# Loads of the modulation's weights on GpSimd's queue instead of SyncE's

## The chip, the cores and the metric

The kernel runs on one core of a Trainium2 chip. The core has TensorE (PE, matrix products), VectorE (DVE), ScalarE (ACT), GpSimd (POOL) and SyncE (SP), which work in parallel, each through its own instructions in a fixed order, and wait for each other on semaphores. Data comes from the chip's memory by DMA; an engine's queue issues a DMA, and the core's 16 DMA engines carry it out. The metric is device time in microseconds (us) of one execution. Everything is in 32-bit floats.

## The reference

One block of a network works on 256 rows of width 2048 in three sublayers. Each sublayer is wrapped in the same way:

```
h = modulate(rms_norm(x, gain_pre), shift, scale)      # h * (1 + scale) + shift
y = rms_norm(fn(h), gain_post)
x = x + weight * (1 + gate) * y
```

The first and the third `fn` are feed-forward layers, `(silu(h @ w_gate) * (h @ w_up)) @ w_down`, with an inner width of 5632. The second is a mixer: `h @ w_in`, then a pooling branch on 512 columns and a recurrent branch (24 heads of size 64, with decay) on the rest, joined and multiplied by `w_out`.

The shifts, scales and gates are the modulation. They are nine vectors of 2048 (three for each sublayer), all from one product of a single row with a large matrix:

```
mod = (silu(c) @ w_ada + b_ada).reshape(B, 3, 3, D_MODEL)
```

`w_ada` is 2048 x 18432, 151 MB. Nothing in it depends on `x`, so its columns can be read at any time before the vector they make is needed.

## The kernel before

**Matrix products.** Each 32-bit weight tile is split into a high and a low part (`split`, lines 173 to 184): ScalarE writes `hi` (line 179), VectorE writes `lo = raw - hi` (line 180), and TensorE sums three products of the parts (lines 189 to 191, 196 and 197, or 523 to 525). A weight tile, `raw`, is loaded by `load` (line 169) on SP's queue, mostly 1 MB at a time. There are four such buffers in the feed-forward layers and two in the mixer. A buffer is free again when line 180 has read it.

**The modulation.** It does not use TensorE for the large product. `ada_step` (lines 220 to 265) handles a quarter of the 2048 rows of `w_ada` for one task. A task is 1024 columns of one vector (two tasks a vector), except for the first two vectors, shift and scale of the first sublayer, whose tasks hold the same columns of both, in five blocks of growing width. For each group of 128 rows the step loads a tile of 128 x 1024 numbers (512 KB, line 235; for the first two vectors 256 KB pieces, line 238) and VectorE adds it, scaled by `silu(c)`, to an accumulator (line 242 for the first, line 244 for the others). At the end of a task VectorE transposes and sums the accumulator, and small products on TensorE finish it (lines 246 to 265). The tiles are called `ada`; there are four such buffers in the feed-forward layers and two in the mixer.

**When the steps run.** The order of the vectors is set in `begin` (line 1163): `(1, 0)` first, then 2, 4, 3, 5, 7, 6, 8. `ada_end` holds the step at which each one ends, and `ada_pos` is the step that is next; the first two vectors take 20 steps of four row groups, each of the seven others 8 steps. Calls of `tick` (lines 616 and 749) after the loads of weights start a step every so many loads, by the constants `ADA_FFN1`, `ADA_MIXER`, `ADA_OUT`, `ADA_FFN2`; `ada_finish` (line 267) runs the missing steps before a vector is needed.

**Stages.** The first feed-forward layer (to about 800 us) reads most of the modulation beside its own weights. The mixer follows (to about 1400 us), then the second feed-forward layer, which has loads of the modulation only at its start.

**What sets the order.** The program is written as one sequence with priorities. A planner of the framework lays out the order in which each engine and each queue gets its instructions, by these priorities, its own estimates of durations, and free buffers. On the chip each queue then works strictly in this order: SP's queue holds the loads of weights and those of the modulation, and a load that waits for its buffer holds back all loads behind it. ScalarE's queue issues a few small loads. GpSimd's queue issues none.

Of the kernel before, what the change touches and what calls it, by code (L numbers as in the profile page):

```python
# [18 lines left out]
D = 2048  # L19
# [57 lines left out]
class Block:  # L77
# [142 lines left out]
    def ada_step(self, psum):  # L220
        nc = self.nc
        if self.ada_pos == len(self.ada_tasks):
            return
        cols, k0 = self.ada_tasks[self.ada_pos]
        width = cols[0][2]
        (v0, c0, _), (v1, c1, _) = cols
        per = 512 // width
        if k0 == 0:
            self.acc = self.tile(self.accs, [P, 2, width], tag="acc")
        acc = self.acc  # L230
        for kk in range(k0, k0 + 4, per):
            raw = self.tile(self.raws, [P, per, 2, width], tag="ada", bufs=self.ada_bufs)
            w = self.I["w_ada"][kk * P:(kk + per) * P, :].rearrange("(k p) c -> p k c", p=P)
            if (v0, c0 + width) == (v1, c1):
                nc.sync.dma_start(raw.rearrange("p k j c -> p k (j c)"), w[:, :, v0 * D + c0:v0 * D + c0 + 2 * width])
            else:
                for j, (v, c, _) in enumerate(cols):
                    nc.sync.dma_start(raw[:, :, j, :], w[:, :, v * D + c:v * D + c + width])
            for i in range(per):
                ck = self.csilu[:, kk + i:kk + i + 1]  # L240
                if kk + i == 0:
                    self.later(nc.vector.tensor_scalar(acc, raw[:, i], ck, None, ALU.mult))
                else:
                    self.later(nc.vector.scalar_tensor_tensor(acc, raw[:, i], ck, acc, ALU.mult, ALU.add))  # L244
        self.ada_pos += 1
        if k0 == KD - 4:
            n = width // P
            ps = self.tile(psum, [P, 512], tag="mm")[:, :2 * n]
            if v0 != v1:
                for i in range(2 * n):  # L250
                    nc.tensor.matmul(ps[:, i:i + 1], acc[:, i // n, i % n * P:(i % n + 1) * P], self.ones[:, :1],
                                     start=True, stop=True)
            else:

                flip = self.tile(self.raws, [P, 2 * width], tag="ada", bufs=self.ada_bufs)
                nc.vector.transpose(flip, acc.rearrange("p j c -> p (j c)"))
                sums = self.tile(self.small, [P, 2 * n, 4], tag="sums")
                nc.vector.tensor_reduce(sums.rearrange("p k q -> p (k q)"), flip.rearrange("p (b t) -> p b t", t=32),
                                        mybir.AxisListType.X, ALU.add)
                for q in range(4):  # L260
                    nc.tensor.matmul(ps[32 * q:32 * q + 32, :], self.quads, sums[:, :, q], start=True, stop=True)
            for j, (v, c, _) in enumerate(cols):
                for a, m, ap in self.columns("b_ada", v * KD + c // P, n):
                    nc.vector.tensor_tensor(self.mod[:, v, c // P + a:c // P + a + m], ps[:, j * n + a:j * n + a + m],
                                            ap, ALU.add)
# [1000 lines left out]
```

## Time and profile before

| | us |
|---|---|
| median of 3 runs | 2158.49 (2156.7 to 2158.58) |
| the profiled execution | 2157.36 |
| its span | 2155.6 |
| TensorE busy | 2072.4 |
| VectorE busy | 1621.2 |
| ScalarE busy | 1079.1 |
| GpSimd busy | 0.2 |

The profile is of one execution. In its rows L169 is line 169 of the kernel; `lo L180` is the instruction of line 180 that writes the tile `lo`; `SPq` is SP's queue, and `A <- B` in a table of waits means that A waited for B, with the total in us, how often, and the longest. In groups, `x224` is a count, and three numbers with slashes are the shortest, median and longest duration in ns. TensorE's busy time is modelled from its pipelined products. The chain of waits is the work that ended last, followed back step by step to what released it. A row of busy time by stretches gives the length, the busy us and instructions of each engine, the granted TensorE clock, the share of time in which the DMA engines moved data, and GB/s.

### The profile page before, as it was taken

Reading aid. Unit: us, or ns where it says so; the run is one execution under the profiler, and the core shown is the slowest. Engines: PE = TensorE matmul, PEld = TensorE weight load, DVE = VectorE, ACT = ScalarE, POOL = GpSimd, SP = SyncE. Lnnn points to the kernel's source line nnn. Section 1 sums busy time; section 2 is a strip of 40 time slices with the busy share of each in tenths; the row PEclk is TensorE's granted clock in tenths of the full one; section 3 lists DMA queues with packets and bytes.
Section 4 is the critical chain, followed back from the end, with each engine's and each line's share of the span. In section 5 each row is a group of like instructions: output and inputs, shape, how many; then the busy total and the mean of one; then the engine's idle time right before and its main releaser. Section 6 shows DMA issues by size and latency. Waiting matters only on the chain.

```text
span 2155.6 us, 37182 instructions
## 1 busy us (share of the span) xinstructions
PE 2072.4 (96%) x14955; PEld 1802.4 (84%) x14955; DVE 1621.2 (75%) x2523; ACT 1079.1 (50%) x1823; POOL 0.2 (0%) x4
## 2 busy tenths in 40 slices
PE   4999999999999998899999999999999999999998
PEld 3999988888888877888887866799888888888887
DVE  6788898798877778899998877788755555555556
ACT  4534543444433455765656654665434444444453
POOL 0000000000000000000000000000000000000000
PEclk8999999999999999999999979999999999999999
DMA  9999888999888748845644526599755555555553
GB/s 317 359 315 322 289 282 306 323 336 315 304 308 294 277 141 243 258 140 173 192 137 147 182 81 195 169 311 320 254 195 194 180 193 196 187 185 195 194 181 133
DMA packets 316570, 502.31 MB, mean 233 GB/s; under 512 B 12037, under 2 KB 197486, under 8 KB 316142
## 3 DMA queue, kind: packets, MB, share of 16 engines
q1 hardware_dynamic: 314380, 496.32, 68.6%
q10 hardware_dynamic: 2018, 3.62, 0.5%
q8 instruction: 117, 1.92, 0.4%
q14 instruction: 55, 0.45, 0.1%
HBM read 497.77 MB, written 2.12 MB: 232 GB/s over the span
## 4 chain that ended last, share of the span: by engine, by line
PE 83%; DMA 7%; DVE 6%; ACT 3%; issue 2%; SPq 0%; DVEq 0%; ACTq 0%
PE mm L196 21%; PE mm L197 10%; PE mm L191 7%; PE mm L190 7%; PE mm L189 7%; PE mm L523 7%; PE mm L525 7%; PE mm L524 7%; DMA ada<-in_w_ada_dram 5%; DVE lo L180 2%; DVE acc L244 1%; DMA raw<-in_w_in_dram 1%; ACT hi L179 1%; PE sb L1110 1%; PE sb L1145 0%
## 5 line engine op out<-in xcount | busy, mean ns | idle before, releaser
L179 ACT CAST hi<-raw 128x1024 fp32r<-128x1024 f32 (+2 forms) x768 | 694.6, 911 | 780.7 <-PE mm L525 266.9
L180 DVE TENSOR_TENSOR lo<-raw,hi 128x1024 fp32r<-128x1024 f32 (+2 forms) x768 | 796.4, 1048 | 351.6 <-ACT hi L179 348.5
L196 PE MATMUL mm<-hT,hi 128*128 128x512 f32 x1984 | 698.6, 395 | 0.0
L197 PE MATMUL mm<-hT,lo 128*128 128x256 f32 x1984 | 558.3, 281 | 2.4 <-DVE lo L180 2.4
L196 PEld LDWEIGHTS mm<-hT,hi 128*128 128x128 f32 x1984 | 373.8, 188 | 87.9
L244 DVE SCALAR_TENSOR_TENSOR acc<-ada,csilu,acc 128x1024 f32<-128x1024 f32 (+1 forms) x285 | 349.0, 1225 | 96.7 <-DMA ada<-in_w_ada_dram 94.7
L190 PE MATMUL mm<-hT,hi 128*128 128x256 f32 x1376 | 395.0, 288 | 3.4 <-DVE hT L362 3.4
L189 PE MATMUL mm<-hT,hi 128*128 128x256 f32 x1376 | 392.0, 289 | 4.0 <-ACT hT L357 3.8
L191 PE MATMUL mm<-hT,lo 128*128 128x256 f32 x1376 | 393.2, 287 | 0.5 <-DVE lo L180 0.5
L197 PEld LDWEIGHTS mm<-hT,lo 128*128 128x128 f32 x1984 | 372.8, 188 | 3.3 <-DVE lo L180 3.1
L189 PEld LDWEIGHTS mm<-hT,hi 128*128 128x128 f32 x1376 | 260.9, 191 | 10.6 <-ACT hT L357 6.1
L190 PEld LDWEIGHTS mm<-hT,hi 128*128 128x128 f32 x1376 | 261.9, 190 | 9.1 <-DVE hT L362 5.5
L191 PEld LDWEIGHTS mm<-hT,lo 128*128 128x128 f32 x1376 | 261.9, 191 | 4.5 <-DVE lo L180 0.7
L523 PE MATMUL mm<-hi,act 128*128 128x512 f32 (+1 forms) x688 | 264.9, 385 | 0.0
L524 PE MATMUL mm<-lo,act 128*128 128x512 f32 (+1 forms) x688 | 264.5, 384 | 0.0
L525 PE MATMUL mm<-hi,act 128*128 128x512 f32 (+1 forms) x688 | 264.4, 384 | 0.0
L524 PEld LDWEIGHTS mm<-lo,act 128*128 128x128 f32 x688 | 129.3, 188 | 25.9 <-DVE lo L180 0.6
L525 PEld LDWEIGHTS mm<-hi,act 128*128 128x128 f32 x688 | 129.3, 188 | 25.7
L523 PEld LDWEIGHTS mm<-hi,act 128*128 128x128 f32 x688 | 129.3, 188 | 25.6
L641 ACT ACTIVATE silu<-silu 128x512 f32<-128x512 f32 x31 | 19.6, 632 | 58.0 <-DVE silu L640 58.0
L644 ACT CAST act<-silu 128x512 fp32r<-128x512 f32 x31 | 19.2, 618 | 31.1 <-DVE silu L642 31.1
L606 DVE TENSOR_TENSOR act<-act,mm 128x512 f32<-128x512 f32 x48 | 32.2, 681 | 1.8 <-PE mm L191 1.6
(371 smaller groups left out, 1936.2 us busy)
## 6 DMA issues: line engine op xcount, KB each, us to landing
ada<-in_w_ada_dram SPq DMA_DIRECT2D x224, 512.0 KB
raw<-in_ffn_w_down_dram SPq DMA_DIRECT2D x88, 1024.0 KB
raw<-in_ffn_w_gate_dram SPq DMA_DIRECT2D x84, 1024.0 KB
raw<-in_ffn_w_up_dram SPq DMA_DIRECT2D x84, 1024.0 KB
raw<-in_w_in_dram SPq DMA_DIRECT2D x34, 1024.0 KB
ada<-in_w_ada_dram SPq DMA_DIRECT2D x128, 256.0 KB
raw<-in_w_out_dram SPq DMA_DIRECT2D x16, 1024.0 KB
raw<-in_w_in_dram SPq DMA_DIRECT2D x9, 512.0 KB
```

Of the source, the lines that this page charges most:

```text
L179: a = nc.scalar.copy(hi, raw)
L180: d = nc.vector.tensor_tensor(lo, raw, hi.bitcast(F32), ALU.subtract)
L189: nc.tensor.matmul(ps, hi, x[:, 0, :], start=start, stop=False)
L190: nc.tensor.matmul(ps, hi, x[:, 1, :], start=False, stop=False)
L191: nc.tensor.matmul(ps, lo, x[:, 0, :], start=False, stop=stop)
L196: nc.tensor.matmul(ps.rearrange("p a t -> p (a t)"), hi, x.rearrange("p a t -> p (a t)"), start=start, stop=False)
L197: nc.tensor.matmul(ps[:, 0, :], lo, x[:, 0, :], start=False, stop=stop)
L244: self.later(nc.vector.scalar_tensor_tensor(acc, raw[:, i], ck, acc, ALU.mult, ALU.add))
L523: nc.tensor.matmul(ps, x[:, 0, ts], hi, start=start, stop=False)
L524: nc.tensor.matmul(ps, x[:, 0, ts], lo, start=False, stop=False)
L525: nc.tensor.matmul(ps, x[:, 1, ts], hi, start=False, stop=stop)
L606: nc.vector.tensor_tensor(part, part, bank, ALU.add)
```

## The change

`ada_step` chooses the queue for its loads. While the position is before the end of the first two vectors, `(1, 0)`, the loads stay on SP's queue. From then on GpSimd's queue issues them. The tiles, their buffers, the instructions that use them and the places of the steps in the program are as before.

```
         for kk in range(k0, k0 + 4, per):
             raw = self.tile(self.raws, [P, per, 2, width], tag="ada", bufs=self.ada_bufs)
+
+            queue = nc.sync if self.ada_pos < self.ada_end[(1, 0)] else nc.gpsimd
             w = self.I["w_ada"][kk * P:(kk + per) * P, :].rearrange("(k p) c -> p k c", p=P)
             if (v0, c0 + width) == (v1, c1):
-                nc.sync.dma_start(raw.rearrange("p k j c -> p k (j c)"), w[:, :, v0 * D + c0:v0 * D + c0 + 2 * width])
+                queue.dma_start(raw.rearrange("p k j c -> p k (j c)"), w[:, :, v0 * D + c0:v0 * D + c0 + 2 * width])
             else:
                 for j, (v, c, _) in enumerate(cols):
-                    nc.sync.dma_start(raw[:, :, j, :], w[:, :, v * D + c:v * D + c + width])
+                    queue.dma_start(raw[:, :, j, :], w[:, :, v * D + c:v * D + c + width])
```

## The prediction

> **What bounds the kernel now.** I read the page of the profile first, then busy time by stretches of 50 us, then the waits of three places.
>
> ```profile
> PE 2072.4 (96%) x14955; PEld 1802.4 (84%) x14955; DVE 1621.2 (75%) x2523; ACT 1079.1 (50%) x1823; POOL 0.2 (0%) x4
> ...
> PE 83%; DMA 7%; DVE 6%; ACT 3%; issue 2%; SPq 0%; DVEq 0%; ACTq 0%
> ```
>
> TensorE is busy for 96% of the span and holds 83% of the chain that ended last; SP's queue holds 0%. GpSimd does nothing. The change works on the queue that nobody waits for by this account, so the first question is where TensorE is idle at all.
>
> ```profile
> 0.00:50.00 50.00, 18.15 (x91) 15.96 (x92) 33.80 (x61) 20.83 (x34) 0.20 (x4) 0.89 0.93 312
> ...
> 450.00:500.00 50.00, 50.00 (x291) 43.33 (x290) 44.48 (x51) 24.57 (x32) 0.00 (x0) 1.00 0.96 332
> ...
> 650.00:700.00 50.00, 47.55 (x252) 40.23 (x252) 38.77 (x40) 19.05 (x24) 0.00 (x0) 0.97 0.82 288
> ...
> 800.00:850.00 50.00, 43.12 (x309) 36.76 (x308) 43.77 (x95) 33.96 (x77) 0.00 (x0) 1.00 0.73 222
> 850.00:900.00 50.00, 42.46 (x349) 39.76 (x349) 38.73 (x67) 31.30 (x62) 0.00 (x0) 1.00 0.84 268
> ...
> 950.00:1000.00 50.00, 48.98 (x621) 43.23 (x608) 46.50 (x117) 29.58 (x76) 0.00 (x0) 1.00 0.51 156
> ...
> 1400.00:1450.00 50.00, 45.65 (x363) 44.03 (x363) 41.83 (x55) 32.94 (x52) 0.00 (x0) 0.97 0.92 320
> ...
> 1600.00:1700.00 100.00, 100.00 (x557) 86.92 (x556) 53.83 (x58) 45.99 (x57) 0.00 (x0) 1.00 0.58 190
> ```
>
> The columns after the length are busy us of PE, PEld, DVE, ACT and POOL, then the granted clock, the DMA share and GB/s. Of 2155.6 - 2072.4 = 83.2 us without TensorE, 31.9 lie in the first 50 us, where the modulation loads that stay on SP are read. The first feed-forward layer runs at 50.00 of 50 with the DMA engines at 0.96; the second, from 1600 us, at 100 of 100 with no modulation left. The stretches that the change can reach and that are not full are 650 to 700 (2.45 us idle), the mixer's start from 800 to 900 (6.88 + 7.54 = 14.4 us), the rest of the mixer (about 1 us in 50), and the opening of the second feed-forward layer (4.35 us).
>
> **The change, part by part.** These are the loads in question, what issuing them costs SP, and the instruction that consumes them.
>
> ```profile
> ada<-in_w_ada_dram SPq DMA_DIRECT2D x224, 512.0 KB
> ```
>
> ```profile
> L244 DVE SCALAR_TENSOR_TENSOR acc<-ada,csilu,acc x285: 742/1279/1289, 5.9 to 1536.4; 128x1024 f32<-128x1024 f32 x128, 128x512 f32<-128x512 f32 x15
> L235 SPq DMA_DIRECT2D ada<-in_w_ada_dram x224: 327/439/1888, 220.9 to 1524.8; - x112
> L238 SPq DMA_DIRECT2D ada<-in_w_ada_dram x128: 327/422/2020, 1.2 to 203.6; - x128
> L242 DVE TENSOR_SCALAR acc<-ada,csilu x19: 481/748/756, 5.4 to 1472.8; 128x1024 f32<-128x1024 f32 x17, 128x512 f32<-128x512 f32 x2
> ```
>
> All 224 loads of line 235 move (7 vectors of 32); the 128 of line 238, up to 203.6 us, are the first two vectors and stay. So the first 220 us, with their 31.9 idle us, cost the same: 0.
>
> *SP gets shorter.* It loses 224 x 0.439 = 98 us of issuing and what it waited for the modulation's buffers:
>
> ```profile
> SPq L169 <- DVE lo L180: 1031.5, 229, 11.3
> ...
> SPq L235 <- DVE acc L244: 113.0, 42, 19.7
> ```
>
> The weight loads (line 169) wait 1031.5 us for their own buffers to be freed by line 180, nine times as long as SP waits for those of line 235. A weight load that is no longer queued behind a modulation load will in most cases only wait for its own buffer instead. In the feed-forward layers I take 0: TensorE is full there, four weight buffers cover it. If that cover were gone, the 113.0 us would be the ceiling of what weight loads could have been held up.
>
> *The modulation's loads lose their place in the line.* Today they queue behind weights; this shows at 691 us. Below, first the chain of waits (start, length), then VectorE in time.
>
> ```profile
> 682.02 9.06 DMA ada<-in_w_ada_dram
> 691.18 1.28 DVE acc L244
> ```
>
> ```profile
> 679.10 1.28 DVE L244 SCALAR_TENSOR_TENSOR acc<-ada,csilu,acc 128x1024 f32<-128x1024 f32 x1 [1.40 <-DMA ada<-in_w_ada_dram]
> ...
> 691.18 1.28 DVE L244 SCALAR_TENSOR_TENSOR acc<-ada,csilu,acc 128x1024 f32<-128x1024 f32 x1 [3.23 <-DMA ada<-in_w_ada_dram]
> ```
>
> ```profile
> DVE acc L244 <- DMA ada<-in_w_ada_dram: 12.6, 9, 3.2
> ...
> PE mm L197 <- DVE lo L180: 2.4, 1, 2.4
> ```
>
> (The last two rows are the waits from 640 to 700 us.) A 512 KB load issued at 682.02 lands 9.06 us later, since weight loads stand ahead of it in the queue; VectorE, which works in order, stands for 3.23 us before line 244, the split of line 180 behind it is late, and TensorE stops once, for 2.4 us. That is the only stall in the whole feed-forward layer: the 12.6 us of VectorE waits in this stretch cost TensorE 2.4. On a queue of its own the load could go out when line 244 frees its buffer (about 680.4, the end of the row at 679.10) and would share the engines with the weights instead of following them. I count this stall as removed: -2.4 us. If the load comes as late as before, it is 0.
>
> *GpSimd now issues.* No row shows a DMA issued by GpSimd. From below its cost is SP's shortest, 0.327 us, from above SP's longest, 1.888 us (both line 235); I take the middle, 1.1 us, 0.66 more than SP's median, because descriptors made by GpSimd should not be quicker than SP's. In the feed-forward layers four buffers hide it. In the mixer there are two, and loads of line 235 stand on the chain at two places in its start, with weights in between:
>
> ```profile
> 824.04 6.63 DMA raw<-in_w_in_dram
> ...
> 836.33 5.32 DMA ada<-in_w_ada_dram
> ...
> 847.91 5.35 DMA raw<-in_w_in_dram
> ...
> 858.24 6.70 DMA raw<-in_w_in_dram
> ...
> 869.87 4.70 DMA ada<-in_w_ada_dram
> ```
>
> Two links x 0.66 = +1.3 us; the ends are 2 x (0.327 - 0.439) = -0.2 and 2 x (1.888 - 0.439) = +2.9.
>
> By the row above, line 242 does 1024 elements in 748 ns where line 244 takes 1279, so it runs in a faster mode. The Trainium skill (SBUF — State Buffer, "SBUF: two separate sides") says that GpSimd cannot write descriptors while VectorE runs an instruction in a two-port mode, and that this is the reason to keep such loads off GpSimd's queue. By that rule the 17 wide instructions of line 242 would hold descriptors back for at most 17 x 0.748 = 12.7 us, spread over 1300 us; lines 180 and 244 have two SBUF inputs, which the page says does not stop descriptor writing, so by the rule the sum stays. No run here shows it yet.
>
> *The mixer's start.* Weights have two buffers there and wait in both directions:
>
> ```profile
> ACT hi L179 <- DMA raw<-in_w_in_dram: 8.6, 5, 3.9
> ...
> DVE acc L244 <- DMA ada<-in_w_ada_dram: 2.2, 3, 0.9
> ```
>
> ```profile
> SPq L169 <- DVE lo L180: 16.1, 7, 5.3
> SPq L235 <- DVE acc L244: 6.6, 6, 1.4
> ```
>
> These are 850 to 900 us. A weight load goes out when line 180 frees its buffer (16.1 us of waits), and ACT then waits for it to land (8.6): latency counts here, from both ends, with the DMA engines at 0.84. The same bytes move in both kernels, so earlier modulation means later weights. I take 0; the ends are the rivals below.
>
> The sum: -2.4 + 1.3 = -1.1 us, against the profiled execution's own 2157.36 (span 2155.6 and 1.76 around it): 2156.3. The median of the runs, 2158.49, lies 1.13 above that execution, so the forecast on the median is 2157.4. A difference up to 0.2%, 4.3 us, is about what a measurement here can't tell from no change: the forecast is "the same".
>
> **The rivals.**
>
> *Faster: the mixer's start gets its data earlier.* SP's rows in time:
>
> ```profile
> 736.70 37.12 SPq L169 DMA_DIRECT2D raw<-in_ffn_w_down_dram  x8
> 794.93 0.88 SPq L169 DMA_DIRECT2D raw<-in_w_in_dram  x2
> 795.86 0.94 SPq L235 DMA_DIRECT2D ada<-in_w_ada_dram  x2
> ```
>
> ```profile
> 785.00:790.00 5.00, 5.00 (x24) 4.14 (x23) 2.47 (x3) 2.15 (x3) 0.00 (x0) 1.00 0.00 0
> ```
>
> ```profile
> ACT hi L179 <- DMA raw<-in_w_in_dram: 3.8, 3, 2.3
> ```
>
> SP stands in line 169 until 794.93 while the DMA engines do nothing, and two modulation loads stand behind it; GpSimd could send them before, and later ones whenever a buffer is free. ACT's waits for weights there, 3.8 (800 to 850 us, the row above) + 8.6 = 12.4 us, are the ceiling; half of it, 6.2, with the 2.4 at 691 us and no cost of issuing gives 2158.5 - 8.6 = 2149.9. Against it: only if the buffers are free before 794.93, and VectorE's order of lines 180 and 244 decides when the data is used.
>
> *Slower: the modulation takes the engines from the weights where they are late.* In one queue a modulation load issued behind a weight load waits for it; in two queues they share. The place is the mixer's start. One load of 512 KB at 316 GB/s, a middling slice of the first layer in the row below, is about 1.66 us (estimate: 524,288 bytes / 316 GB/s). The weights there go round on two buffers; SP waited for line 180 on 9 + 7 = 16 loads (the 9 are of 800 to 850), so 8 rounds. If each round's weight comes 1.66 us later, that is +13.3 us, less 2.4: 2169.4. It decides once weights land later than line 180 would have freed the other buffer, which at 850 to 900 us they do already (8.6 us of waits). In the feed-forward layers the same sharing is covered: there SP waits on buffers and nothing in the table of 640 to 700 us waits for weights.
>
> ```profile
> SPq L169 <- DVE lo L180: 12.7, 9, 2.4
> ```
>
> ```profile
> GB/s 317 359 315 322 289 282 306 323 336 315 304 308 294 277 141 243 258 140 173 192 137 147 182 81 195 169 311 320 254 195 194 180 193 196 187 185 195 194 181 133
> ```
>
> The Trainium skill (DMA: Bandwidth & Descriptors, "Queues, rings and completion order") says that each DMA engine takes turns between queues packet by packet; the modulation's runs are 4 KB and those of the mixer's weights 1 KB, which by that rule would favour the modulation while both are queued, and so speaks for this rival.
>
> *The order changes elsewhere.* The planner lays out every engine's order anew. If it lets the four instructions of line 244 that belong to one step run together (4 x 1.279 = 5.1 us) ahead of a split, a stall like that at 691 us can come once for each of the 7 moved vectors: 7 x 2.4 = +17, 2175.
>
> *It doesn't do what it says:* the loads are held by line 244 and not by SP, nothing moves, 2158.5. This counts with the forecast.
>
> **How the numbers follow.** Forecast, with "nothing moves": 0.42. Mixer's start faster: 0.30. Weights squeezed: 0.18. New order worse: 0.10. The cases within 4.3 us are the first, the faster is the second, the slower the last two: faster 0.30, same 0.42, slower 0.28. The likeliest one's own range is 2154.2 to 2161; the range for 8 in 10 reaches down to the faster rival, with 2 us beyond it, 2148, and up to the squeezed weights, 2169. Above it is left the new order and some of the squeezed case, below it little.
>
> **What would show it.** Right if POOL shows 224 DMA issues and SP's rows of line 235 are gone; if the 2.4 us stall near 691 us is gone; if TensorE's idle time from 800 to 900 us stays within 3 us of 14.4 and the full stretches stay full. The faster rival shows as DMA traffic between 780 and 795 us and fewer ACT waits for weights; the squeezed case as weight loads of the mixer that take over 7 us, and a longer stretch before 900; the new order as stalls of lines 197 or 524 on line 180. The forecast is wrong if GpSimd's issue takes several us, so that line 244 waits longer than the 94.7 us it waits now:
>
> ```profile
> DVE acc L244 <- DMA ada<-in_w_ada_dram: 94.7, 64, 4.3
> ```

## The result, and the profile after

| | before | after |
|---|---|---|
| median of the runs (us) | 2157.59 | 2176.2 |
| lowest and highest | 2156.32 to 2158.58 | 2174.86 to 2178.8 |
| ratio, 95% interval | | 1.0088, 1.0073 to 1.0104 |
| the profiled execution, its span | 2157.36, 2155.6 | 2176.0, 2174.0 |

The change makes the kernel 18.6 us slower, where 2157.4 was forecast and 2169 was the upper end. Behind line 232 the changed kernel's lines have numbers two higher: 235 is now 237, 244 is 246, 1112 is 1114, 1121 is 1123, 1146 is 1148.

The page of the changed kernel: engines, chain by engine, a group, the rows of the issues.

```profile
PE 2077.5 (96%) x14955; PEld 1808.1 (83%) x14955; DVE 1618.3 (74%) x2523; ACT 1079.5 (50%) x1823; POOL 118.6 (5%) x228
...
GB/s 306 355 317 326 314 298 391 376 374 360 338 205 194 177 141 267 216 158 170 178 143 167 189 83 127 161 348 343 185 194 193 193 183 194 185 194 193 189 182 133
...
PE 79%; issue 7%; DVE 5%; DMA 5%; ACT 2%; POOL 0%; SPq 0%; DVEq 0%; POOLq 0%; ACTq 0%
...
L246 DVE SCALAR_TENSOR_TENSOR acc<-ada,csilu,acc 128x1024 f32<-128x1024 f32 (+1 forms) x285 | 349.0, 1224 | 37.9 <-DMA ada<-in_w_ada_dram 35.5
...
L237 POOL DMA_DIRECT2D ada<-in_w_ada_dram x224 | 118.4, 529 | 1388.2 <-DVE acc L246 591.8
...
ada<-in_w_ada_dram POOLq DMA_DIRECT2D x224, 512.0 KB, 6.4
```

The change did what it says: 224 issues moved, each takes GpSimd 0.529 us, and VectorE's waits for these loads fell from 94.7 to 35.5 us. Nevertheless TensorE holds 79% of the chain, down from 83%. Outside its busy time lie 2174.0 - 2077.5 = 96.5 us, 13.3 more than before; and the same 14955 products take 5.1 us longer: the mean granted clock is 0.980, where it was 0.984.

Now the same stretches as before the change (length; busy us of PE, PEld, DVE, ACT, POOL; clock, DMA share, GB/s).

```profile
450.00:500.00 50.00, 50.00 (x290) 43.39 (x290) 49.97 (x56) 24.76 (x34) 9.37 (x18) 1.00 1.06 374
...
650.00:700.00 50.00, 50.00 (x274) 42.74 (x273) 26.44 (x29) 21.47 (x26) 0.00 (x0) 1.00 0.58 189
...
800.00:850.00 50.00, 42.47 (x298) 35.83 (x297) 41.70 (x82) 30.69 (x67) 4.75 (x9) 1.00 0.72 215
850.00:900.00 50.00, 40.34 (x296) 38.40 (x296) 36.34 (x59) 30.44 (x60) 6.33 (x12) 0.86 0.82 258
...
1000.00:1100.00 100.00, 91.55 (x1150) 78.61 (x1150) 85.04 (x218) 60.19 (x158) 7.92 (x15) 1.00 0.58 182
```

```profile
1000.00:1100.00 100.00, 99.44 (x1321) 84.03 (x1320) 90.09 (x246) 68.28 (x185) 0.00 (x0) 1.00 0.53 164
```

(The last row is of before.) In the first feed-forward layer the modulation runs far ahead: 374 GB/s at 450 to 500 us where it was 332, and GpSimd issues no modulation load at all from 650 to 700. The stall at 691 us is gone, 50.00 of 50. The mixer has become worse: 850 to 900 us has 2.1 us less of TensorE and a clock of 0.86, and 1000 to 1100, which was full, now has 8.45 us idle.

To add this up I use points that both traces have: the first product of line 523 (525) in the first layer, the first product of the mixer (line 189), the ends of line 1146 (1148), which finishes a pair of heads of the mixer's recurrence (12 pairs), and the first product of the second feed-forward layer. These are the rows of pairs 1, 2, 3 and 6, before and after (start, length).

```profile
965.68 0.41 DVE L1146 TENSOR_TENSOR y<-t,sb 128x256 f32<-128x256 f32 x1
996.86 0.41 DVE L1146 TENSOR_TENSOR y<-t,sb 128x256 f32<-128x256 f32 x1
1030.88 0.42 DVE L1146 TENSOR_TENSOR y<-t,sb 128x256 f32<-128x256 f32 x1
...
1128.78 0.40 DVE L1146 TENSOR_TENSOR y<-t,sb 128x256 f32<-128x256 f32 x1
```

```profile
973.36 0.42 DVE L1148 TENSOR_TENSOR y<-t,sb 128x256 f32<-128x256 f32 x1
1003.49 0.40 DVE L1148 TENSOR_TENSOR y<-t,sb 128x256 f32<-128x256 f32 x1
1046.74 0.41 DVE L1148 TENSOR_TENSOR y<-t,sb 128x256 f32<-128x256 f32 x1
...
1149.59 0.41 DVE L1148 TENSOR_TENSOR y<-t,sb 128x256 f32<-128x256 f32 x1
```

| stretch (us) | before | after | |
|---|---|---|---|
| start to line 523 | 283.9 | 287.1 | +3.2 |
| line 523 to the mixer's first product | 524.5 | 519.4 | -5.1 |
| A: mixer's first product to pair 1 | 157.7 | 167.3 | +9.6 |
| B: pair 1 to pair 6 | 163.1 | 176.2 | +13.1 |
| C: pair 6 to the second feed-forward layer | 272.3 | 266.6 | -5.7 |
| from there to the end | 754.1 | 757.4 | +3.3 |

The sum is +18.4, the difference of the spans. Of the first row's +3.2, 2.4 are idle time of TensorE in the first 60 us, where no load has moved; this row differs between the kernels below by as much. The last row's +3.3 lies in the opening of the second feed-forward layer: up to the first product of line 196 there it is 79.1 us before and 82.2 after, and from there to the end 675.0 and 675.2. The loss is mainly A and B. So the first layer gains what the forecast hoped for, and more, and the mixer loses three times that.

In B, pair 2 to pair 3 took 34.0 us and takes 43.3. This is VectorE there, after the change.

```profile
1006.85 1.28 DVE L246 SCALAR_TENSOR_TENSOR acc<-ada,csilu,acc 128x1024 f32<-128x1024 f32 x1
...
1008.65 1.28 DVE L246 SCALAR_TENSOR_TENSOR acc<-ada,csilu,acc 128x1024 f32<-128x1024 f32 x1
...
1013.15 1.28 DVE L246 SCALAR_TENSOR_TENSOR acc<-ada,csilu,acc 128x1024 f32<-128x1024 f32 x1 [1.55 <-DMA ada<-in_w_ada_dram]
...
1014.95 0.23 DVE L1114 COPY SV<-sb 64x64 f32<-64x64 f32 x1
...
1015.97 1.28 DVE L246 SCALAR_TENSOR_TENSOR acc<-ada,csilu,acc 128x1024 f32<-128x1024 f32 x1 [0.57 <-DMA ada<-in_w_ada_dram]
...
1020.43 1.28 DVE L246 SCALAR_TENSOR_TENSOR acc<-ada,csilu,acc 128x1024 f32<-128x1024 f32 x1 [1.70 <-DMA ada<-in_w_ada_dram]
...
1021.83 0.23 DVE L1114 COPY SV<-sb 64x64 f32<-64x64 f32 x1
```

```profile
PE sb L1123 <- DVE SV L1114: 4.2, 2, 2.6
```

```profile
PE sb L1121 <- DVE SV L1112: 0.5, 1, 0.5
```

Five accumulations come within 15 us, on two buffers, and wait three times for their load. Small copies of the recurrence (line 1114, 0.23 us) stand in line behind them, and TensorE waits for these copies (line 1123, small products that read them). The last two fences are TensorE's waits from pair 2 to pair 3, after and before: 4.2 us and 0.5 us. TensorE is idle for 43.25 - 37.43 = 5.8 us in that stretch; the rest of the 9.3 us that it is longer is mostly other products that now stand in it, 480 in place of 449. Over the whole mixer (A, B and C) TensorE's idle time has grown from 31.7 to 43.3 us, and its waits for these copies from 2.0 to 10.3 us (the rows, after and before):

```profile
PE sb L1123 <- DVE SV L1114: 10.3, 8, 2.6
```

```profile
PE sb L1121 <- DVE SV L1112: 2.0, 4, 0.6
```

An idea for a cause is at hand: VectorE's order. Compared instruction by instruction, 904 of VectorE's 2510 instructions, 9990 of TensorE's 13142 and 1184 of ScalarE's 1800 have the same place in both programs. The planner moved instructions on every engine, though the diff touches only a queue. (One instruction that moves shifts the places of all those it passes. In the longest sequence that both orders have in common stand 1843 of VectorE's, 12215 of TensorE's and 1542 of ScalarE's.) The count of accumulations between the points shows it too (VectorE's busy us and instructions of line 244 before, of line 246 after, from 780 us to pair 1, from 780 us to pair 6, and from there to 1400 us).

```profile
780.00:965.68 185.68, 33.21 (x26) 0.99 0.65 199
...
780.00:1128.78 348.78, 56.22 (x44) 1.00 0.59 181
1128.78:1400.00 271.22, 30.71 (x24) 0.93 0.49 155
```

```profile
780.00:973.36 193.36, 37.13 (x29) 0.96 0.65 198
...
780.00:1149.59 369.59, 65.16 (x51) 0.97 0.60 182
1149.59:1400.00 250.41, 21.73 (x17) 0.93 0.46 146
```

Of the mixer's 68, 44 lay before the end of pair 6, and now 51. They have moved forward, into A and B, which lose, and out of C, which gains.

### The profile page after: what moved, and what is told of

It is laid out like the page before. It is cut to its first block, busy times and chain, and to the rows that moved or that the text cites. A ratio compares the mean times of both kernels' runs of the same rounds, so it can differ in the third digit from the quotient of the medians.

```text
span 2174.0 us, 37386 instructions
## 1 busy us (share of the span) xinstructions
PE 2077.5 (96%) x14955; PEld 1808.1 (83%) x14955; DVE 1618.3 (74%) x2523; ACT 1079.5 (50%) x1823; POOL 118.6 (5%) x228
## 4 chain that ended last, share of the span: by engine, by line
PE 79%; issue 7%; DVE 5%; DMA 5%; ACT 2%; POOL 0%; SPq 0%; DVEq 0%; POOLq 0%; ACTq 0%
PE mm L196 21%; PE mm L197 11%; PE mm L525 8%; PE mm L527 8%; PE mm L526 8%; PE mm L190 6%; PE mm L191 5%; PE mm L189 5%; DMA ada<-in_w_ada_dram 4%; DVE lo L180 1%; DVE acc L246 1%; DMA raw<-in_w_in_dram 1%; ACT hi L179 0%; PE mm L253 0%; DMA x<-in_x_dram 0%
## 5 line engine op out<-in xcount | busy, mean ns | idle before, releaser
L246 DVE SCALAR_TENSOR_TENSOR acc<-ada,csilu,acc 128x1024 f32<-128x1024 f32 (+1 forms) x285 | 349.0, 1224 | 37.9 <-DMA ada<-in_w_ada_dram 35.5
L189 PEld LDWEIGHTS mm<-hT,hi 128*128 128x128 f32 x1376 | 263.3, 193 | 14.7 <-ACT hT L359 6.5
L237 POOL DMA_DIRECT2D ada<-in_w_ada_dram x224 | 118.4, 529 | 1388.2 <-DVE acc L246 591.8
L526 PEld LDWEIGHTS mm<-lo,act 128*128 128x128 f32 x688 | 129.3, 188 | 25.4
```

The lines of the kernel that those rows point to most:

```text
L189: nc.tensor.matmul(ps, hi, x[:, 0, :], start=start, stop=False)
L237: queue.dma_start(raw.rearrange("p k j c -> p k (j c)"), w[:, :, v0 * D + c0:v0 * D + c0 + 2 * width])
L526: nc.tensor.matmul(ps, x[:, 0, ts], lo, start=False, stop=False)
```

## The experiments

### The queue alone, and the order alone

Two things changed together: the queue, and the order that the planner makes of it. They can be had apart. A dependency from each instruction to the next of its engine, without a semaphore, holds that engine in a given order (line 282 of the kernel before has the function `in_order` that makes it):

```
-        Block(ctx, tc, I, out).run()
+        block = Block(ctx, tc, I, out)
+        first = {i.name for i in nc.all_instructions()}
+        block.run()
+        hold_order(block, nc, first)
...
+def hold_order(block, nc, first):
+    made = {i.name: Made(i) for i in nc.all_instructions() if i.name not in first}
+    for names in json.loads(zlib.decompress(base64.b85decode(ORDER))).values():
+        block.in_order([made[f"I-{n}"] for n in names if f"I-{n}" in made])
```

`ORDER` is the list of an engine's instructions as the other program has them.

The first kernel is the changed one with VectorE, ScalarE, TensorE and SP's remaining loads held in the order of before. The second is the kernel before, all on SP, with VectorE, ScalarE and TensorE held in the order of after.

> The changed kernel with VectorE, ScalarE, TensorE and SP's remaining loads held in the order of the kernel before; only the queue of the 224 loads is GpSimd's. Theory 1 (sharing of the DMA engines by two queues makes the mixer's weights late): slower by 10 to 18 us, 2168 to 2176, with ScalarE's waits for w_in weights from 800 to 900 us again near 24 us instead of 12. Theory 2 (the planner's new order of the engines costs the time): 2151 to 2160, so within 3 us of before or faster by the 4.4 us that the first feed-forward layer gained. Theory 3 (issuing on GpSimd is slow, 0.28 us of wait and 0.53 of issue against 0.44): at most 4 us slower.

> The kernel before, all loads on SP's queue, with VectorE, ScalarE and TensorE held in the order of the changed kernel. Theory 1 (sharing): within 4 us of before, 2154 to 2162. Theory 2 (order): as slow as the changed kernel, 2170 to 2180, or slower, since in SP's queue the modulation's loads come later than that order was laid out for.

Measured: the queue alone 2154.28 against 2159.72 us, ratio 0.9979 (0.9962 to 0.9996). The order alone, on SP's queue, 2271.52 us, 1.0518 (1.0482 to 1.0553). So the queue alone costs nothing, and the loss goes when the order does. The second kernel's time is not the price of the order in the changed kernel: of the 124.0 us by which its span (2279.6) is longer than before, 64.8 lie between line 523 and the mixer, where the changed kernel gains. The order is laid out for loads that come early, and on SP's queue they don't: VectorE's accumulations wait 125.4 us for them, where it was 94.7.

I ran the queue alone a second time, beside other kernels.

> The changed kernel with the four orders held as before the change, a second time, now with as many rounds as an effect of 0.2% needs. Theory (the queue alone makes the kernel slightly faster): ratio 0.997 to 0.999, interval below 1. Rival (the first result, 0.9979 with its upper end at 0.9996, was chance): 0.999 to 1.001.

Measured: 2152.26 against 2156.08 us, 0.9989 (0.9975 to 1.0002). The interval reaches 1; with both runs the queue alone is worth 0.1 to 0.2%, at the border of what can be told from nothing. Its profile:

```profile
PE 2067.5 (96%) x14955; PEld 1799.1 (84%) x14955; DVE 1625.9 (76%) x2523; ACT 1080.1 (50%) x1823; POOL 119.0 (6%) x228
```

```profile
991.81:1025.92 34.11, 33.81 (x449) 28.00 (x449) 30.52 (x84) 24.61 (x68) 3.18 (x6) 1.00 0.60 185
```

The second row is pair 2 to pair 3: 34.1 us, as before the change, with the loads on GpSimd's queue (six issues in it). By stretches: line 523 to the mixer 519.4 (-5.1), A 160.1 (+2.4), B 163.3, C 272.8. The first run's profile has 519.3, A 163.2, B 162.6, C 270.7, so two profiles of the same kernel differ by 3 us in A.

### Which stage

The queue changes in one stage only, the other stages' loads stay on SP; the order is the planner's.

```
-            queue = nc.sync if self.ada_pos < self.ada_end[(1, 0)] else nc.gpsimd
+            queue = nc.sync if self.ada_pos < self.ada_end[(1, 0)] or self.stage not in POOL_STAGES else nc.gpsimd
```

> GpSimd's queue issues the modulation's loads of the first feed-forward layer alone; those of the mixer and of the second layer are on SP's queue. All theories put the loss into the mixer (15 to 17 us between 806 and 1400 us), so here the gain of the first layer is left: the 2.4 us stall near 691 us gone, 2151 to 2157. If it is 2165 or more, the loss does not come from what the queue is in the mixer, but from how far the modulation has got when the mixer starts.

> GpSimd's queue issues the modulation's loads of the mixer alone; those of the first and second feed-forward layers are on SP's queue. Theories 1 and 2 both: the mixer's loss without the first layer's gain and without the second layer's 3 us, 2169 to 2177. Theory 3: under 2162.

Measured: the first feed-forward layer alone 2156.93 us against 2159.72, 0.9986 (0.997 to 1.0001); the mixer alone 2176.83, 1.007 (1.0045 to 1.0095). The mixer carries the loss. In the profile of the latter A is 168.8 and B 179.2 us, as after the full change; in that of the former A is 158.2 and B 162.2, as before.

The planner's order in the former also differs from before, in 449 places of VectorE, all among its first 667 instructions. I held this order and gave all loads to GpSimd:

> The changed kernel with all four orders held as they are laid out when only the first feed-forward layer's modulation goes to GpSimd (0.9986 there). Against the order of before, VectorE differs in 449 places, ScalarE in 31, TensorE in 41, SyncE in none. Theory (the loss is the mixer's new order; the first layer's new order costs nothing): ratio 0.996 to 0.999, as with before's order. Rival (the first layer's order with more room for the modulation is worth something by itself): under 0.996. If over 1.003, the first layer's order does cost once the mixer's loads come from GpSimd.

Measured: 2154.48 against 2156.08 us, 0.9991 (0.9978 to 1.0005). The first layer's new order neither costs nor brings anything; what costs is the mixer's.

### Is it the order itself, or waiting for loads in that order?

Five accumulations in a row are 6.4 us of VectorE whether their data is there or not. In both kernels below the mixer's loads of the modulation are taken away but one; VectorE, ScalarE and TensorE are held, in the first in the order of after, in the second in that of before.

```
+            skip = self.split_ahead and self.one is not None
+            raw = self.one if skip else self.tile(self.raws, [P, per, 2, width], tag="ada", bufs=self.ada_bufs)
```

> The changed kernel with VectorE, ScalarE and TensorE held in its own order, but in the mixer only the first tile of the modulation is loaded; the others are left out, and line 246 adds this one tile every time (so the vectors made there are not those of the reference). No load of the modulation can be late in the mixer, and none shares the DMA engines. Theory 2a (the new order is fine in itself, but the loads land later than it was laid out for, so VectorE waits): the 15 to 17 us of the mixer go, 2155 to 2162. Theory 2b (the places that the instructions have in the new order cost the time, whatever the loads do): at most 5 us go, 2168 to 2176.

> The same with the three engines held in the order of the kernel before, so that the two orders are compared without any load of the modulation in the mixer but the first (left out as in the run beside it). Theory 2a: within 4 us of that run. Theory 2b: 10 to 18 us faster than it. Against the run with the order of before and all loads on GpSimd's queue (2154.3) the sharing of the DMA engines in the mixer is what can be gained: 0 to 8 us, 2146 to 2154.

Measured: order of after 2150.31 us against 2155.08, 0.9979 (0.9956 to 1.0002); order of before 2140.29, 0.9931 (0.9912 to 0.995). Without the mixer's loads the new order costs 0.0048, some 10 us, give or take 0.003 by the two intervals. With them it costs 1.0088 - 0.9979 = 0.0109, or 0.0099 by the second run: 21 to 24 us. The first time lies below both of its ranges, and the second is 10.0 us faster than the first, at the lower end of theory 2b. The stretches show more closely where it lies. In order of after against order of before, A is 153.7 against 148.0 without the loads (+5.7) and 167.3 against 160.1 with them (+7.2); B is 169.3 against 162.4 (+6.9), and 176.2 against 163.3 (+12.9); C is 263.0 against 269.4 (-6.4), and 266.6 against 272.8 (-6.2). So the new order costs the mixer 6.2 us without the loads and 13.9 with them: a little under half of that is the place of the instructions, the rest the loads that these places make late. Another part lies outside the mixer, in the opening of the second feed-forward layer up to line 196, where all four kernels have their loads: 83.0 against 76.8 us, and 82.2 against 77.1. There the accumulations end earlier too, 98.6 us after the layer's first product in the changed kernel, 129.8 with the order held. I did not follow what TensorE loses there.

The first two answers also price the loads themselves: in the order of before, the mixer's loads cost 0.9979 - 0.9931, some 10 us, or 12 by the second run.

### One engine held

If VectorE's order is the matter, holding VectorE alone should be enough; if TensorE's is, holding that.

> The changed kernel with VectorE alone held in the order of the kernel before; the planner lays out TensorE, ScalarE and SP around it. If it is VectorE's order that costs the time: 2151 to 2160, as with all engines held. If it is TensorE's or ScalarE's: 2166 to 2178.

> The changed kernel with TensorE alone held in the order of the kernel before; the planner lays out VectorE, ScalarE and SP. If it is TensorE's order that costs the time: 2151 to 2160. If it is VectorE's (the places of lines 244 and 246): 2166 to 2178. In between if both take part.

Measured: VectorE held 2167.23 us against 2155.08, 1.005 (1.0035 to 1.0065); TensorE held 2187.07, 1.0141 (1.0121 to 1.0161). The first time lies in the range that was named for TensorE's or ScalarE's order, the second above both ranges, so neither engine's order is the matter alone. VectorE's is worth over a third of what the order costs; TensorE held to an order that VectorE doesn't follow makes it worse. With VectorE held, pair 2 to pair 3 is back where it was:

```profile
1002.89:1036.87 33.98, 33.70 (x449) 27.99 (x449) 30.69 (x84) 24.67 (x68) 3.18 (x6) 1.00 0.62 187
```

B is 164.1 us; but A is still 168.5, and C is 277.4, where it is 272.8 with all four held.

### Two engines held

> The changed kernel with the orders of VectorE and TensorE held as before the change; ScalarE then keeps 1725 of 1800 places and SyncE 518 of 520, by the planner. Theory A (the order's cost lies in VectorE and TensorE together, VectorE alone gave back half of it): the time goes to that with everything held, ratio 0.996 to 1.000. Theory B (the order's cost lies in ScalarE's casts and SyncE's loads, which follow VectorE's order): 75 places of ScalarE off still cost, ratio 1.003 or more, as with VectorE alone (1.0050).

> The changed kernel with the orders of VectorE and ScalarE held as before the change; all 520 of SyncE's places then agree, and TensorE differs in 516 of 13142. Theory A (TensorE's own places are the other half): ratio stays near 1.005, since TensorE's order is free as it was with VectorE alone. Theory B (ScalarE and SyncE are the other half): ratio 0.996 to 1.000. If both this and the run with VectorE and TensorE held come to 0.998, then what is left over after VectorE is a matter of any second engine that ties the others down.

Measured, beside the second run of the queue alone (0.9989): VectorE and TensorE held 2160.34 against 2156.08 us, 1.0027 (1.0012 to 1.0042); VectorE and ScalarE 2158.06, 1.002 (1.0007 to 1.0034). Neither expectation is met: each second engine gives back two fifths or half of what was left, 0.0023 and 0.0030 of 0.0061, and 0.3 to 0.4% stays. The stretches show where (all of the changed kernel):

| held as before | ratio | A | B | C |
|---|---|---|---|---|
| none | 1.0088 | 167.3 | 176.2 | 266.6 |
| TensorE | 1.0141 | 170.4 | 183.3 | 273.8 |
| VectorE | 1.005 | 168.5 | 164.1 | 277.4 |
| VectorE, TensorE | 1.0027 | 165.1 | 163.0 | 271.4 |
| VectorE, ScalarE | 1.002 | 166.9 | 163.0 | 272.8 |
| all four, first run | 0.9979 | 163.2 | 162.6 | 270.7 |
| all four, second run | 0.9989 | 160.1 | 163.3 | 272.8 |

B hangs on VectorE alone. A, the start of the mixer, comes nearest to before when all four are held: with VectorE and TensorE held only 75 of ScalarE's 1800 places and 2 of SP's 520 differ, and A is still 1.9 to 5 us longer than with all four. Two profiles of one kernel differ by 3 us in A, so for this step the ratios (1.0027 and 1.002 against 0.9979 and 0.9989) say more than A does. Which of those instructions does it is open.

A possible reason why A is so touchy is seen in its waits, 800 to 850 and 850 to 900 us, after the change:

```profile
ACT hi L179 <- DMA raw<-in_w_in_dram: 10.5, 6, 3.3
...
SPq L169 <- DVE lo L180: 18.2, 9, 3.7
...
ACT hi L179 <- DMA raw<-in_w_in_dram: 13.1, 4, 4.8
...
DVE lo L180 <- ACT hi L179: 11.5, 9, 3.1
...
SPq L169 <- DVE lo L180: 17.0, 5, 5.7
```

The rows form a ring: SP waits for `lo` to free one of two buffers, ScalarE waits for SP's load, `lo` waits for ScalarE. What comes late in it can come round again; no run here takes the ring apart. But the waits of ScalarE for weights, 23.6 us here against 12.4 before, are not the price by themselves. With all four orders held they are 11.8 + 7.7 = 19.5 in the second run, where A is 160.1, and in the first run 14.7 + 8.8 = 23.5, as long as here, where A is 163.2 and the ratio 0.9979 (in that kernel a helper's line 102 stands for every operation):

```profile
ACT hi L102 <- DMA raw<-in_w_in_dram: 14.7, 9, 3.9
...
ACT hi L102 <- DMA raw<-in_w_in_dram: 8.8, 4, 3.6
```

## Why the prediction was wrong

**The step that failed** stands in the part on the mixer's start: "The same bytes move in both kernels, so earlier modulation means later weights. I take 0". It is a sentence on transfers, and it takes the mixer's instructions to stay in their places. They didn't: with the places held, the sum comes near (0.9979 and 0.9989, -4.5 and -2.4 us, where -1.1 was worked out), though its terms are others, -5.1 in the first layer and up to +5.5 in A. With the planner's places the mixer loses 17 us (A, B and C together).

Two signs that were named didn't tell this. TensorE's idle time from 800 to 900 us is 17.2, within 3 us of 14.4, as named for a right forecast; and lines 197 and 526 (524 before) never wait for line 180, as named for a new order. The sign that told was that 1000 to 1100 us didn't stay full. The rest of the mixer wasn't "about 1 us in 50" either: 1250 to 1300 us had 6.1 idle before the change. The sum didn't use it.

**The stall at 691 us: right, and too small.** It is gone, in every kernel whose first layer loads through GpSimd. Removed were not 2.4 but 5.1 us. The rest is the clock, in the trace of before:

```profile
690.00:695.00 5.00, 2.55 (x13) 2.00 (x12) 3.82 (x4) 0.00 (x0) 0.00 (x0) 0.93 0.56 196
695.00:700.00 5.00, 5.00 (x23) 4.25 (x23) 5.00 (x7) 2.71 (x4) 0.00 (x0) 0.73 0.40 135
700.00:705.00 5.00, 5.00 (x31) 4.36 (x30) 4.67 (x7) 1.51 (x3) 0.00 (x0) 1.00 0.94 321
```

After the stall TensorE does 23 products in 5 us, with the clock at 0.73, where it does 31 at 1.00: eight products, 8 x 5/31 = 1.3 us, lost while it counts as busy. In the 5 us before, 13 products took 2.55 us of busy time where 31 take 5.00: 0.45 us. With the idle 2.4 that makes 4.2 of the 5.1. (The clock column says the same: 5 x (0.07 + 0.27) = 1.7 us.) The Trainium skill (TensorE: Matmul & The Clock Gate, Part 1: The HAM clock gate (the "warmup" mystery)) says that the clock halves after an idle window of about 3.4 us and comes back after a busy one of the same length. The slow time here, some 3 us, agrees with the second half of this; the idle time before it was 2.4 us and already enough. Such a gap isn't always enough: in the changed kernel a wait of 2.60 us for one of the small copies left the clock at 1.00.

```profile
1015.23 0.34 PE L1123 MATMUL sb<-SV,bt 128*64 128x64 f32 x4 [2.60 <-DVE SV L1114]
```

```profile
1010.00:1015.00 5.00, 2.63 (x31) 2.03 (x30) 3.42 (x8) 3.46 (x10) 0.80 (x2) 1.00 0.85 279
1015.00:1020.00 5.00, 4.77 (x44) 4.26 (x45) 3.03 (x10) 3.94 (x13) 0.78 (x2) 1.00 1.03 307
```

**GpSimd's issue: the price was half of mine, and no effect shows.** GpSimd holds 0% of the chain, and its issue is 0.529 us, not 1.1, so the two links would be +0.2 us, not +1.3. By the rule of the Trainium skill quoted there (SBUF — State Buffer, "SBUF: two separate sides") lines 180 and 244 were not to hold GpSimd up. The trace agrees: from 450 to 500 us VectorE is busy for 49.97 of 50 us, and GpSimd's 18 issues take 9.37 / 18 = 0.52 us each.

**SP's shorter queue: 0, right.** SP's waits for line 180 rose from 1031.5 to 1259.7 us. These 228 us are near the 113.0 + 98 that it no longer spends on line 235, and TensorE stayed full.

```profile
SPq L169 <- DVE lo L180: 1259.7, 229, 39.2
```

**The rivals.** *The mixer's start gets its data earlier*: no. GpSimd has no loads to send before 793 us; its row waits 208.36 us for line 428, a sum of VectorE's at the end of the first layer, and the mixer's buffers are made only for that stage. From 785 to 790 no data moves, as before.

```profile
793.27 1.05 POOL L237 DMA_DIRECT2D ada<-in_w_ada_dram  x2 [208.36 <-DVE base L428]
816.67 0.53 POOL L237 DMA_DIRECT2D ada<-in_w_ada_dram  x1 [22.36 <-DVE acc L246]
```

```profile
785.00:790.00 5.00, 5.00 (x24) 4.14 (x23) 3.50 (x5) 1.82 (x2) 0.00 (x0) 1.00 0.00 0
```

*Weights squeezed*: its signs are there, ScalarE waits for the mixer's weights nearly twice as long, and a weight load on the chain takes 8.98 us where over 7 was named. But the waits are as long when the order is held (23.5 us in the first of the two runs), and then A is 2.4 to 5.5 us longer, not 13.3, and the kernel as a whole is not slower. (A single load over 7 us was no sign: before the change one on the chain takes 7.91 us, at 907.43.) The rule of packets taken in turn (DMA: Bandwidth & Descriptors, "Queues, rings and completion order", in the Trainium skill) spoke for this rival; that the weights wait longer agrees with it, and the price it was to explain didn't come.

```profile
875.02 8.98 DMA raw<-in_w_in_dram
```

*The order changes elsewhere* was the case, at 0.10. Its mechanism, accumulations in a row ahead of work that TensorE needs, is what 1006 to 1022 us shows; its 17 us is near the 18.6. But its place was wrong, and so the agreement in size is chance: I put it in the feed-forward layers, ahead of the splits, once for each vector. In the first of them four buffers and a full TensorE hide even 29 accumulations run ahead (at 600 us 187 of line 246 are done, where 158 of line 244 were). It costs in the mixer, where TensorE waits for VectorE's small copies and the row of accumulations waits for its loads, and some 5 us in the second feed-forward layer's opening, though there are four buffers there too.

What I could have seen: the front text says that the planner lays out every engine's queue by free buffers and its own estimates. When a load comes, by its estimate, depends on the queue it stands in. The chance of 0.10 treated as an accident what the program's description makes the rule, and the range ended where this case began.

## What to carry to other kernels

Where a planner sets the order, a change of a queue can change every engine's order: price the new order first, or hold the old one and measure the two apart, as here (queue 0.998 to 0.999, order +1%). A queue that promises data earlier lets the planner put its consumers earlier, and an engine that works in order makes everything behind them wait; look at which of its short instructions feed the bound engine, first of all in the stage with the fewest buffers. And a stall of TensorE can cost more than its idle time, so look at the clock behind it and count the slow products too.

## What the runs showed of the hardware

I hadn't expected the clock to drop for some 3 us after only 2.4 us without products. It doubled the price of that stall, while a gap of 2.60 us elsewhere cost no clock. The slower clock is a large share of the order's price: of the 25.4 us between the changed kernel's span with the planner's order (2174.0) and with the order held (2148.6), 2077.5 - 2067.5 = 10.0 are busy time of the same 14955 products.

GpSimd's issue of a 512 KB load was cheaper than I thought and hardly varied, whatever VectorE did (shortest, median, longest in ns; start of the first and the last; the row is below). The changed kernel moved 374 to 391 GB/s in three slices of the first layer (from 326 us), where the kernel before had 306 to 336. The second queue alone doesn't give this: with the order of before held, two queues moved 312 to 329 there.

```profile
L237 POOL DMA_DIRECT2D ada<-in_w_ada_dram x224: 527/527/662, 207.5 to 1506.5; - x112
```
